# Weights that begin 64 and 192 bytes past the moving tiles: an encoder block on one Trainium2 core

## Chip, cores and metric

The kernel runs on one core of one Trainium2 chip (trn2). The metric is the device time of one execution in microseconds, taken as the median of several runs.

## What is computed

The reference is one layer of an encoder for 512 tokens of width 1024. Two token mixers, a differential attention and a neighbourhood attention, are merged by gates; then comes a feed-forward part with 2816 hidden channels. The change touches the feed-forward part, and of that its first half:

```python
x = x + rmsnorm(merged @ w_out[l], post_mix_w[l])
h = rmsnorm(x, pre_ffn_w[l])
f = (jax.nn.silu(h @ w_gate[l]) * (h @ w_up[l])) @ w_down[l]
x = x + rmsnorm(f, post_ffn_w[l])
```

All arrays are float32. The products h @ w_gate and h @ w_up are 512 x 1024 by 1024 x 2816 each.

## The kernel before

**Products in three parts.** TensorE is fed with float32r tiles. Every operand is cut into a high part (a rounded copy, made by ScalarE) and a low part (the rest, made by a subtraction on VectorE), and a product is the sum of three matmuls: high by high, high by low, low by high (`mm3`, lines 215 to 218, and lines 1109 to 1112). Each matmul has a load of 128 x 128 stationary values ahead of it, so loads and matmuls alternate one to one.

**Weights.** The class `Weights` loads a unit of weights (128 x 1024 float32, 512 KB) into one of five `raw` tiles, cuts it into the high and low part, and puts these where a place function says. Most units use `place_w` (line 197): one of four slots of the tag "w", each of 8192 bytes a partition, the high part in the first half and the low part in the second. Slots are used in turn; a slot is free again when the last matmul that reads it is done.

**Feed-forward, first blocks (UF).** Lines 1051 to 1075 multiply the first 256 gate and up columns in the usual way, 4 units with 2 halves of 256 tokens: 192 matmuls with 256 moving columns. The weights are stationary, the transposed h is moving. It stands in the two tiles of the tag "hT", which are named `Q` here (lines 925 to 929): `Q[g, n]` holds the channels 512g to 512g+511 of the tokens 256n to 256n+255, high and low part behind each other. The second half of UF needs the second half of Q, which `to_Q(h2[3], 3)` and `t_sums(1)` finish while the first half runs.

**Pair stage.** The other 20 blocks (10 gate, 10 up; 256 columns each) are computed with seven products instead of eight, in the manner of Strassen and Winograd. `pair_steps` (lines 64 to 128) makes from two weight units the stationary operands: A11 and A12 (step s0, one "w" slot, tile name "m0"), S2 and S1 (s2, one "w" slot, "s21"), S3 and S4 (s4, written over `Q[0, 1]`, which isn't needed any more, "s34"), and A22 (s5, a tile of 4096 bytes from the pool "u", "a22"). `pair_pl` (line 1033) says where each goes. The moving operands are the parts of Q (`B11`, `B21`, `B22`) and the sums T1 to T4, which are tiles of 4096 bytes of the pool "u". Each of the seven products is 12 matmuls (4 channel blocks by 3), so a block is 84 matmuls, and the stage 20 x 84 = 1680, all with 128 x 128 stationary values and 256 moving columns. For A11, A12 and A22 the low part is made by ScalarE (minus the high part) and an accumulating DMA from the queue of POOL that adds the raw weights (lines 71 to 74). The steps of the next block are dealt out between the products of the present one.

**Order.** From line 520 on a scheduler puts the instructions of each engine in order at build time; that order is then fixed.

**Addresses.** The program of before has these first bytes in a partition: slots of "w" at 18304, 26496, 34688 and 42880 (8192 each); "raw" from 51072; the 18 slots of "u" from 71552 (4096 each); the small tiles in between end at 146816, and there begin the two "hT" tiles (146816 and 163200, 16384 each). All of these are 128 modulo 256 and 384 modulo 512. Inside the tiles, parts and blocks of columns begin at multiples of 512 bytes. So every stationary operand of the pair stage begins at the same address modulo 256 as every moving one. The constants, `ident` (the moving operand of transposes) among them, begin elsewhere.

Of the kernel before, what the change touches and what calls it, by code (L numbers as in the profile page):

```python
# [9 lines left out]
F32R = mybir.dt.float32r  # L10
# [4 lines left out]
S = 512  # L15
# [17 lines left out]
def dram(ap, offset, pattern):  # L33
    return bass.AP(tensor=ap.tensor, offset=ap.offset + offset, ap=pattern)
# [143 lines left out]
def block_kernel(ctx: ExitStack, tc: tile.TileContext, x, pre_mix_w, w_in,  # L178
# [6 lines left out]
    wp = ctx.enter_context(tc.tile_pool(name="w", bufs=4))  # L185
# [7 lines left out]
    hp = ctx.enter_context(tc.tile_pool(name="hT", bufs=2))  # L193

    W = Weights(nc, rp, 5)

    def place_w():
        t = wp.tile([128, 2, 1024], F32R, tag="w", name="w")
        return t[:, 0, :], t[:, 1, :]

    def place_pool(pool):
        def go():
# [5 lines left out]
    def U(dt, shape, name, pool=None):  # L208
        return (pool or up).tile(shape, dt, tag="u", name=name)

    def cols128(w, c0, kn=KD):
        n = w.shape[1]
        return dram(w, c0, [[n, 128], [128 * n, kn], [1, 128]])
# [20 lines left out]
    for nm, c0 in (("vb", 2560), ("va", 1024)):  # L234
        for j in range(4):
            n = w_in.shape[1]
# [5 lines left out]
    def add_qk(br, i):  # L242
        qc = (1536 if br == "b" else 0) + 128 * i
        UQ[br, i, "q"] = W.add(cols128(w_in, qc), (8, 128), place_w)
        UQ[br, i, "k"] = W.add(cols128(w_in, qc + 512), (8, 128), place_w)
# [3 lines left out]
    def add_branch(nm, w, j):  # L249
        n = w.shape[1]  # L250
        src = dram(w, 256 * j, [[n, 128], [128 * n, 4], [1, 256]])
        UBR[nm, j] = W.add(src, (4, 256), place_w)
# [20 lines left out]
    UF = {}  # L273
    for m in range(2):
        for nm, w in (("g", w_gate), ("u", w_up)):
            UF[nm, m] = W.add(cols128(w, 128 * m), (8, 128), place_w)
    UP = {}
    pair_place = Late1()
    for j in range(1, KF // 2):
# [45 lines left out]
    ps_t = stk_ps.enter_context(tc.tile_pool(name="ps_t", bufs=2, space=PSUM))  # L325
    ps_o = stk_ps.enter_context(tc.tile_pool(name="ps_o", bufs=1, space=PSUM))

    hT = [hp.tile([128, 4, 2, S], F32R, tag="hT", name="hT") for _ in range(2)]
    def to_hT(h, b, dst, pool, tag):
        for g in range(2):  # L330
            tb = pool.tile([128, 4, 128], F32, tag=tag, name="tb")
            for k in range(4):
                kk = 4 * g + k
                nc.tensor.transpose(tb[:, k], h[:, 128 * kk:128 * kk + 128], ident)
            hi = dst[g][:, :, 0, 128 * b:128 * b + 128]
            lo = dst[g][:, :, 1, 128 * b:128 * b + 128]
            nc.scalar.activation(hi, tb, AF.Copy)
            nc.vector.tensor_sub(lo, tb, hi.bitcast(F32))
# [551 lines left out]
    for m in range(8):  # L890
# [16 lines left out]
        t = U(F32R, [128, 2, 512], "mg")  # L907
# [13 lines left out]
    for b in range(NB):  # L921
        t = U(F32, [128, D], "x2")
        nc.sync.dma_start(t, tok(x, b))
        x2.append(t)
    Q = {}
    for n in range(2):
        q = hp.tile([128, 2, 2, 4, 256], F32R, tag="hT", name="Q")
        for g in range(2):
            Q[g, n] = q[:, g]
    HR = {}  # L930

    def to_Q(h, b):
# [98 lines left out]
        F.append(f)  # L1031

    def pair_pl(what):
        if what == "a22":
            t = U(F32R, [128, 2, 512], "w22")
            return t[:, 0], t[:, 1]
        if what == "s34":

            return tuple(Q[0, 1][:, n].rearrange("p a b -> p (a b)") for n in range(2))
        return place_w()  # L1040

    pair_place.fn = pair_pl
    pairs = [UP[nm, j] for j in range(1, KF // 2) for nm in ("g", "u")]
# [12 lines left out]
    for half in range(2):  # L1056
        cs = slice(256 * half, 256 * half + 256)
        for m in range(2):
            for nm in ("g", "u"):
# [3 lines left out]
                for k in range(KD):  # L1063
# [3 lines left out]
                    q = Q[k // 4, half]  # L1067
# [111 lines left out]
    for b in range(NB):  # L1179
        f_split()  # L1180
        t = U(F32, [128, D], "x2")
        nc.sync.dma_start(t, x2d[b])
        x2.append(t)
    for b in range(NB):
# [6 lines left out]
        for n in range(2):  # L1191
            c = slice(512 * n, 512 * n + 512)
# [71 lines left out]
```

## Time and profile before

| | us |
|---|---|
| three runs | 753.49, 755.47, 755.78 |
| median | 755.47 |
| the profiled execution | 753.81 |
| its span, from the first to the last instruction | 752.0 |
| attention, gates and output projection, to | 398.6 |
| first feed-forward blocks (UF), to | 422.9 |
| pair stage, to | 625.0 |
| down projection and end, to | 752.0 |

The stages are told by the line numbers in the order of time: lines 216 to 218 with Q and w from 398.64 on, lines 1109 to 1112 from 422.96 to 625.2. The profile names a matmul by its line, and by out<-in with the buffer numbers left out: `b<-Th,w` is a matmul into a PSUM tile b that reads Th (moving, the high part of a T) and w (stationary). The A22 tile (`w22`) shows as w too. A matmul's duration in the trace holds the time that its results take to come out; matmuls overlap. What a matmul costs in a stream is the distance between the starts of two that follow each other.

### The profile page before, as it was taken

What the parts mean: (1) busy time and instruction counts of PE and PEld (TensorE: products, weight loads), DVE (VectorE), ACT (ScalarE), POOL (GpSimd) and SP (SyncE); (2) the same over time, 40 slices, a digit from 0 to 9 for tenths busy, and PEclk for the clock granted to TensorE, in tenths of its full rate; (3) what the DMA queues carried; (4) which work ended last, traced back from release to release, by engine and by line L of the source; (5) the groups of instructions that cost most, each with busy time, mean ns of one, the idle gap of its engine ahead of it and who ended that gap; (6) DMA issues with size and microseconds to landing.
All of it is one profiled execution on the core that took longest, in us unless ns stands there. A gap on an engine that the chain in (4) does not pass through costs nothing. (4 is left out here: it accounts for less than half of the span.)

```text
span 752.0 us, 11240 instructions
## 1 busy us (share of the span) xinstructions
PE 738.1 (98%) x4368; PEld 654.0 (87%) x4368; DVE 481.1 (64%) x840; ACT 377.2 (50%) x612; POOL 82.4 (11%) x129
## 2 busy tenths in 40 slices
PE   8999999999999999999999999999999999999996
PEld 7887888877888888887889999999999998888884
DVE  5625688888776633565467987777778879232333
ACT  6414665665666732453224865666666656222211
POOL 1001001122330000000011111111111110000000
PEclk9999999999999999999999999999999999999998
DMA  9437645333311222354714677887867872443112
GB/s 254 155 95 208 162 119 162 99 98 98 98 57 30 84 84 85 112 199 137 168 56 141 140 190 172 189 195 187 190 155 180 193 225 92 139 168 111 58 40 72
DMA packets 102582, 101.49 MB, mean 135 GB/s; under 512 B 3537, under 2 KB 85473, under 8 KB 102530
## 3 DMA queue, kind: packets, MB, share of 16 engines
q1 hardware_dynamic: 96080, 82.82, 38.2%
q0 software_dynamic: 6448, 17.97, 11.9%
q8 instruction: 34, 0.56, 0.3%
q14 instruction: 18, 0.15, 0.1%
q10 hardware_dynamic: 2, 0.00, 0.0%
HBM read 74.56 MB, written 4.19 MB: 105 GB/s over the span
## 5 line engine op out<-in xcount | busy, mean ns | idle before, releaser
L153 DVE TENSOR_TENSOR w<-raw,w 128x1024 fp32r<-128x1024 f32 x67 | 82.1, 1226 | 83.9 <-ACT w L147 83.2
L147 ACT ACTIVATE w<-raw 128x1024 fp32r<-128x1024 f32 x67 | 70.4, 1054 | 61.9 <-PE b L218 51.7
L216 PE MATMUL mm<-hT,w 128*128 128x512 f32 x256 | 100.8, 394 | 0.3 <-DVE v L391 0.3
L217 PE MATMUL mm<-hT,w 128*128 128x512 f32 x256 | 99.9, 390 | 0.0
L218 PE MATMUL mm<-hT,w 128*128 128x512 f32 x256 | 99.8, 390 | 0.0
L1109 PE MATMUL b<-Th,w 128*128 128x256 f32 x240 | 67.9, 283 | 0.0
L1111 PE MATMUL b<-Tl,w 128*128 128x256 f32 x240 | 67.9, 283 | 0.0
L1112 PE MATMUL b<-Th,w 128*128 128x256 f32 x240 | 67.9, 283 | 0.0
L216 PEld LDWEIGHTS mm<-hT,w 128*128 128x128 f32 x256 | 48.1, 188 | 10.3 <-DVE v L391 0.7
L218 PEld LDWEIGHTS mm<-hT,w 128*128 128x128 f32 x256 | 48.1, 188 | 10.3
L217 PEld LDWEIGHTS mm<-hT,w 128*128 128x128 f32 x256 | 48.1, 188 | 9.3
L216 PE MATMUL b<-w,fh 128*128 128x512 f32 x144 | 56.0, 389 | 0.0
L217 PE MATMUL b<-w,fh 128*128 128x512 f32 x144 | 56.0, 389 | 0.0
L218 PE MATMUL b<-w,fl 128*128 128x512 f32 x144 | 56.0, 389 | 0.0
L74 POOL DMA_DIRECT2D w<-raw x40 | 34.5, 862 | 174.3 <-ACT w L73 161.8
L1111 PEld LDWEIGHTS b<-Tl,w 128*128 128x128 f32 x240 | 46.1, 192 | 0.0
L1112 PEld LDWEIGHTS b<-Th,w 128*128 128x128 f32 x240 | 46.1, 192 | 0.0
L1109 PEld LDWEIGHTS b<-Th,w 128*128 128x128 f32 x240 | 46.1, 192 | 0.0
L1112 PE MATMUL b<-Q,w 128*128 128x256 f32 x160 | 45.4, 284 | 0.2 <-DMA w<-raw 0.2
L1109 PE MATMUL b<-Q,w 128*128 128x256 f32 x160 | 45.3, 283 | 0.0
L1111 PE MATMUL b<-Q,w 128*128 128x256 f32 x160 | 45.3, 283 | 0.0
L976 ACT ACTIVATE junk<-b 128x512 f32<-128x512 f32 x16 | 9.6, 597 | 61.6 <-PE b L218 56.8
(230 smaller groups left out, 1892.7 us busy)
## 6 DMA issues: line engine op xcount, KB each, us to landing
raw<-in_w_in_dram SPq DMA_DIRECT2D x40, 512.0 KB, 4.4
raw<-in_w_gate_dram SPq DMA_DIRECT2D x22, 512.0 KB, 4.3
raw<-in_w_up_dram SPq DMA_DIRECT2D x22, 512.0 KB, 4.7
raw<-in_w_down_dram SPq DMA_DIRECT2D x22, 512.0 KB, 3.3
w<-raw POOLq DMA_DIRECT2D x20, 512.0 KB, 5.7
K<-K SPq DMA_DIRECT2D x24, 256.0 KB, 3.1
w<-raw POOLq DMA_DIRECT2D x20, 256.0 KB, 5.1
x<-in_x_dram SPq DMA_DIRECT2D x8, 512.0 KB, 8.1
```

The lines of the kernel that those rows point to most:

```text
L74: nc.gpsimd.dma_start(lo, src, accum_op=ALU.add)
L147: self.nc.scalar.activation(hi, raw, AF.Copy)
L153: (engine or self.nc.vector).tensor_sub(lo, raw, hi.bitcast(F32))
L216: nc.tensor.matmul(bank, sh, mh, start=first, stop=False)
L217: nc.tensor.matmul(bank, sh, ml, start=False, stop=False)
L218: nc.tensor.matmul(bank, sl, mh, start=False, stop=last)
L976: nc.scalar.activation(junk, bs, AF.Square, scale=1.0 / 32.0, accum_out=ss[:, n:n + 1])
L1109: nc.tensor.matmul(bank[c], sh[:, k], th[:, k], start=opens and k == 0, stop=False, **kw)
L1111: nc.tensor.matmul(bank[c], sh[:, k], tl[:, k], start=False, stop=False, **kw)
L1112: nc.tensor.matmul(bank[c], sl[:, k], th[:, k], start=False, stop=k == 3, **kw)
```

## The change

No instruction is added or taken away. A slot of "w" grows by 256 bytes to 8448, an "hT" tile by 256 bytes to 16640. For the four UF units and for m0 and s21 of the pair stage, the high part begins 16 elements (64 bytes) into the slot and the low part 1072 elements (4288 bytes, 192 modulo 256). All other users of "w" have the high part at 0 and the low part at 4096, as before. Inside the two Q tiles the two groups of channels stand 2112 elements (8448 bytes, 0 modulo 256) apart, for n = 0 in the reverse order; S3 and S4 go to 16 and 1072 elements from the start of the tile for n = 1. A22 keeps its tile from "u". So modulo 256 all moving operands stay where they were, the high parts of the stationary ones of UF and of the pair stage begin 64 bytes and the low parts 192 bytes past them, and A22 begins level with them. All tiles behind the "w" slots move by 1024 bytes; as a slot is now 33 x 256 bytes, the second and fourth slot, and the second "hT" tile, begin 256 bytes off the others modulo 512. The last byte used goes from 226560 to 228096.

```diff
-    def place_w():
-        t = wp.tile([128, 2, 1024], F32R, tag="w", name="w")
-        return t[:, 0, :], t[:, 1, :]
+    def place_w(a=0, b=1024):
+
+        t = wp.tile([128, 2048 + 64], F32R, tag="w", name="w")
+        return t[:, a:a + 1024], t[:, b:b + 1024]
...
-            UF[nm, m] = W.add(cols128(w, 128 * m), (8, 128), place_w)
+            UF[nm, m] = W.add(cols128(w, 128 * m), (8, 128), lambda: place_w(16, 1072))
...
-    hT = [hp.tile([128, 4, 2, S], F32R, tag="hT", name="hT") for _ in range(2)]
+    hT = [hp.tile([128, 4160], F32R, tag="hT", name="hT")[:, :4096]
+          .rearrange("p (k a t) -> p k a t", k=4, a=2) for _ in range(2)]
...
-        q = hp.tile([128, 2, 2, 4, 256], F32R, tag="hT", name="Q")
+        q = hp.tile([128, 4160], F32R, tag="hT", name="Q")
         for g in range(2):
-            Q[g, n] = q[:, g]
+
+            c = 2112 * (1 - g) if n == 0 else 2112 * g
+            Q[g, n] = q[:, c:c + 2048].rearrange("p (a k t) -> p a k t", a=2, k=4)
+            if (g, n) == (0, 1):
+                place34 = q[:, 16:16 + 1024], q[:, 1072:1072 + 1024]
...
         if what == "s34":
-
-            return tuple(Q[0, 1][:, n].rearrange("p a b -> p (a b)") for n in range(2))
-        return place_w()
+            return place34
+        return place_w(16, 1072)
```

## Rows read from the trace of the kernel before

**Rows 1.** The page, busy time of each engine, share of the span, instructions.

```profile
PE 738.1 (98%) x4368; PEld 654.0 (87%) x4368; DVE 481.1 (64%) x840; ACT 377.2 (50%) x612; POOL 82.4 (11%) x129
```

**Rows 2.** Table by stage: stretch, its length, each engine's busy time (instructions), clock, DMA.

```profile
398.60:422.90 24.30, 24.12 (x201) 23.87 (x201) 22.26 (x36) 15.29 (x25) 3.79 (x5) 1.00 0.50 135
422.90:625.00 202.10, 201.90 (x1682) 201.69 (x1682) 160.13 (x242) 127.62 (x170) 32.66 (x38) 1.00 0.79 188
625.00:752.00 127.00, 119.95 (x530) 99.00 (x529) 46.46 (x51) 32.98 (x44) 2.18 (x4) 0.98 0.29 95
```

**Rows 3.** Timeline, pair stage: start, duration, engine, line, what; one block to the next.

```profile
524.24 0.28 PE L1109 MATMUL b<-Q,w 128*128 128x256 f32 x1
...
534.33 0.28 PE L1109 MATMUL b<-Q,w 128*128 128x256 f32 x1
...
534.57 0.28 PE L1112 MATMUL b<-Q,w 128*128 128x256 f32 x1
```

**Rows 4.** Timeline, down projection, matmuls with 512 columns, first and last of 31.

```profile
699.90 0.39 PE L216 MATMUL b<-w,fh 128*128 128x512 f32 x1
...
706.70 0.39 PE L216 MATMUL b<-w,fh 128*128 128x512 f32 x1
```

**Rows 5.** Timeline, a weight load in the same stretch of the pair stage.

```profile
524.25 0.19 PEld L1111 LDWEIGHTS b<-Q,w 128*128 128x128 f32 x1
```

**Rows 6.** Timeline, the first matmuls of UF, the first two and the twelfth.

```profile
398.64 0.28 PE L216 MATMUL b<-Q,w 128*128 128x256 f32 x1
398.75 0.28 PE L217 MATMUL b<-Q,w 128*128 128x256 f32 x1
...
399.95 0.28 PE L218 MATMUL b<-Q,w 128*128 128x256 f32 x1
```

**Rows 7.** Timeline, matmuls with 256 columns in the attention stage.

```profile
169.02 0.28 PE L707 MATMUL o<-pl,v 128*128 128x256 f32 x1
169.13 0.29 PE L706 MATMUL o<-ph,v 128*128 128x256 f32 x1
169.26 0.28 PE L707 MATMUL o<-pl,v 128*128 128x256 f32 x1
169.37 0.28 PE L706 MATMUL o<-ph,v 128*128 128x256 f32 x1
```

**Rows 8.** Timeline, matmuls with 512 columns after other work, the first three and the sixth.

```profile
182.83 0.39 PE L216 MATMUL mm<-hT,w 128*128 128x512 f32 x1
183.06 0.40 PE L217 MATMUL mm<-hT,w 128*128 128x512 f32 x1
183.30 0.39 PE L218 MATMUL mm<-hT,w 128*128 128x512 f32 x1
...
183.99 0.39 PE L218 MATMUL mm<-hT,w 128*128 128x512 f32 x1
```

**Rows 9.** Four transposes: timeline (merged), and their group (busy us, mean ns).

```profile
182.16 0.60 PE L784 MATMUL t<-ident,p 128*128 128x128 f32 x4
...
L784 PE MATMUL t<-ident,p 128*128 128x128 f32 x64 | 9.9, 274 | 0.0
```

**Rows 10.** Groups of the page: count, busy us, mean ns, idle before.

```profile
L216 PE MATMUL mm<-hT,w 128*128 128x512 f32 x256 | 100.8, 394 | 0.3 <-DVE v L391 0.3
...
L216 PE MATMUL b<-w,fh 128*128 128x512 f32 x144 | 56.0, 389 | 0.0
```

**Rows 11.** The two waits of TensorE in the stretch (timeline), and the chain between them.

```profile
411.47 0.39 PE L217 MATMUL b<-Q,w 128*128 128x256 f32 x1 [0.18 <-DVE Q L943]
432.21 0.39 PE L1112 MATMUL b<-Q,w 128*128 128x256 f32 x1 [0.20 <-DMA w<-raw]
...
425.56 6.61 DMA w<-raw
```

**Rows 12.** The accumulating DMAs: one issue (timeline), and landing times of all 40.

```profile
521.13 0.86 POOL L74 DMA_DIRECT2D w<-raw  x1 [6.15 <-ACT w L73]
...
DMA to landing us min/median/max: 3.9/5.6/6.9
```

## Prediction

> **What bounds the kernel now.** I read the page's busy shares first. TensorE is busy 98% of the span [rows 1]. Then the table by stage: the granted clock is 1.00 there, so the upper of its two levels, 2.4 GHz; and in the stretch that the change touches, 398.6 to 625 us, TensorE is idle for 0.4 us of 226.4, and the weight loads fill as much of the time [rows 2]. VectorE (79% of the pair stage), ScalarE (63%) and the DMA engines (0.79) have room. So the stage costs its number of matmuls times the distance from one matmul's start to the next, and nothing but that distance, the pitch, can be won or lost there in any amount.
>
> The pitch comes from start times. From the first matmul of one gate or up block at 524.24 to the same one of the next block at 534.33 lie 84 matmuls: 10.09 / 84 = 0.1201 us; 534.33 to 534.57 are two single steps of 0.12 [rows 3]. In the stage of the down projection, 30 steps with 512 columns take 706.70 - 699.90 = 6.80 us, 0.2267 each [rows 4]. 256 more columns thus cost 106.6 ns, 0.416 ns each, one column per cycle of 2.4 GHz. What 256 columns need alone is 106.6 ns; the other 13.5 ns come with every matmul, at 512 columns (226.7 - 213.2 = 13.5) as at 256.
>
> These 13.5 ns are what the change aims at. During a matmul the weights of the next one are loaded: a load starts within 0.01 us of a matmul's start [rows 3, 5]. Both read SBUF. By the layout of the kernel before, every stationary and every moving float32r tile of the pair stage begins at the same address modulo 256, so here the two reads always start in step; the trace before holds no sustained run at another offset.
>
> **Does the pitch depend on anything but the column count?** Yes, and this is my reason to expect an effect. The same 256-column form does 0.11 for its first step after the 512-column stage and 1.31 / 11 = 0.1191 over the first eleven [rows 6]; in the attention stage three steps in a row are 0.11, 0.13 and 0.11 [rows 7]. After other work the 512-column form does 0.23, 0.24 and three more of 0.23 in the mean (0.232 over the five) before it falls to its lasting 0.2267, with no wait between [rows 8]. A fixed charge for changing weights would not wander by 10 ns; two streams that meet more or less often, according to how they stand to each other, would. An offset moves exactly that standing.
>
> Four transposes of 128 columns show the floor: the row spans 0.60 us, the last one lasts 0.274, so three steps take 0.326, 109 ns each [rows 9]. Their moving part needs only 128 x 0.416 = 53 ns, so 109 ns is the weight load's own pace, and no offset can bring a stream of load and matmul below it.
>
> **The change, part by part.** No instruction is added, removed or moved to another engine. All costs are start addresses.
> 1. New offsets in the pair stage: 1680 matmuls (20 blocks of 84; the window in rows 2 has two of the stage before besides) less the 240 on A22, whose tile stays as it was, so 1440; and the 192 matmuls of the first two feature blocks (UF), together 1632. The price of an offset of 64 or 192 bytes is in no row. Its ends are 109 ns (11 less than now, rows 9) and 125 ns (5 more: the step of 0.13 in rows 7 between two of 0.11, taken at the low end of its rounding). Between them I take 115 ns, 5 less than now: the nearest rows for the same form are the first steps of 0.11 in rows 6 and 7, which are lower than 120 but not sustained, so I take half of the way to the floor.
> 2. Not all of the 1632 can give their 5 ns to the end. The 97 UF matmuls ahead of 411.47 (the first half of 96 and one more) end in a wait for VectorE's chain to Q (0.18 us now); that chain doesn't hang on them, so what they win turns into waiting [rows 11]. Behind it, 169 shifted matmuls up to 432.21 (95 of UF, 74 of the pair stage) run against ScalarE and the accumulating DMAs on POOL's queue: the wait at 432.21 is for such a DMA, issued at 425.56 and there 6.6 us later [rows 11]. That chain starts when TensorE frees a weight slot, so it moves along in part; I count half. Counted in full are 1440 + 192 - 97 - 169 = 1366; with half of 169 it is 1450. 1450 x 5 ns = 7.25 us.
> 3. Slots of 8448 bytes: the offsets of the other stages stay 0 modulo 256, but every second weight slot moves by 256 modulo 512. About half of the 3 x 256 feature matmuls on w and of the 3 x 144 of the down stage [rows 10] are met, 600. No row isolates this; if they ran 0.230 instead of 0.2267, as in rows 8, it would be 3.3 ns x 600 = 2 us, and I know no reason against the opposite sign. Taken at 0, both ends kept.
> 4. The addresses that ScalarE, VectorE and the DMA write: their instructions move as much as before. The accumulating DMA is the only one with little cover at the start (point 2). Later it has plenty: the one issued at 521.13 takes 6.9 us at the longest, so it is there by 528.0, and its low parts are first used by the third matmul of the next block at 534.57 [rows 3, 12]; 6 us are left, and a block that is 0.4 us shorter takes none of this cover away. SyncE's queue gets no new wait.
> 5. VectorE needs 160.13 / 202.1 of the pair stage; if the stage fell to 195, 82%, and at the floor of 109 ns 87%. It doesn't become the bound.
>
> Sum: against the profiled execution, 753.81 us (span 752.0 and 1.8 around it), 753.81 - 7.25 = 746.6. The median of the three runs, 755.47, lies 1.66 above that execution, so the forecast is 748.2.
>
> **A rule that speaks against it.** The Trainium skill, page "SBUF — State Buffer", section "Who interferes with whom", gives TensorE two independent read ports, one for the moving operand and one for the weights, and says that it never waits on anyone; by this no address can matter, and the sum would be 755.5. The page "TensorE: Matmul & The Clock Gate", "Back-to-back issue gap", puts the step at N/2.4 + 2.5, so 109.2 ns for 256 columns, an estimate from that page; the trace has 120.1, and doesn't agree. The wandering steps of rows 6 to 8 don't either.
>
> **The rivals.**
> - *No effect.* The 13.5 ns is the same for 256 and 512 columns [rows 3, 4], as a fixed charge per change of weights would be, and the wandering is only the settling of a pipeline after a break. Then any offset gives 120 ns and the change does nothing: 755.5, 753.5 to 757.5 with point 3. Against it: rows 6 to 8.
> - *All of it goes.* The meetings vanish and the weight load alone sets the pace, 109 to 110 ns: 10.5 x 1450 = 15.2 us, 740.2; with all 1632 and 11 ns, 18 us, 737.5. For it: the transposes hold 109 [rows 9]. Against: in rows 6 and 7 each step of 0.11 has a longer one behind it, and the mean stays at 0.119.
> - *Slower: a worse standing.* The settled pitch at offset 0 could be a good one, and the new offsets put the load where the moving read runs into it longer, at each matmul. Rows 8 speak for it: there the unsettled 512-column steps are longer than the settled one; rows 6 and 7 speak against, since at 256 columns they average less than 120. It decides from 121.4 ns on (1632 x 1.4 ns = 2.3 us). No cover exists, as TensorE has no idle time; at 124 ns it is 1632 x 4 = 6.5 us, 762.0; at 122.5, 4.1 us, 759.6.
>
> **How the numbers follow.** A measurement of this kernel tells about 0.3%, 2.3 us, from no change. Forecast (pitch 111 to 118.4, 743 to 753): 0.42. All of it: 0.18. No effect: 0.22. Slower: 0.18. Faster is 0.42 + 0.18 = 0.60, same 0.22, slower 0.18. For the range I go down to 738, which leaves out 0.06 of the floor case, and up to 760, which leaves out 0.10 of the slower case. The likeliest case's own range is 743 to 753.
>
> **What would show it.** Right: between equal matmuls of two blocks 84 steps take about 9.7 us instead of 10.09; the blocks on A22 (12 matmuls each, offset unchanged) still go at 0.12, right beside blocks at less; weight loads keep their 0.19 us; the down stage keeps 0.2267; the wait for Q at 411.5 grows to some 0.7 us and the one for the DMA at 432 to about 0.5. Steps of 0.12 everywhere would show the no-effect rival; steps of 0.11 everywhere the floor; steps of 0.12 and 0.13 mixed, the slower one. The prediction is wrong if TensorE starts to wait in the pair stage (then the next bound was nearer than points 4 and 5 say), or if the 512-column stages change their step (point 3).

## The result, and the profile after

The changed kernel takes 749.5 us (median of 4 runs, 748.3 to 750.0) against 754.5 for the kernel before (4 runs). The medians lie 5.0 us apart, 0.7%; the ratio of the runs is put at 0.992, with a 95% interval of 0.990 to 0.994. Its profiled execution took 748.33 us with a span of 746.6, 5.5 less than the one of before.

The table by stage, with the borders of the changed kernel's own trace (same columns as rows 2; the first stretch is UF, the second the pair stage, the third the rest):

```profile
398.81:422.55 23.74, 22.97 (x202) 22.77 (x201) 21.86 (x36) 14.74 (x25) 3.79 (x5) 1.00 0.49 134
422.55:619.61 197.06, 195.41 (x1683) 193.44 (x1682) 160.43 (x243) 128.00 (x172) 32.67 (x38) 1.00 0.81 190
619.61:746.60 126.99, 119.86 (x530) 98.91 (x528) 46.46 (x51) 32.90 (x44) 2.18 (x4) 0.99 0.30 100
```

UF falls from 24.3 to 23.7 us, the pair stage from 202.1 to 197.1, the rest stays. TensorE now idles for 1.65 us of the pair stage, where it idled for 0.2.

Now the steps (timeline, columns as in rows 3). First the 24 matmuls of S2 and S1 in one block, then the 12 of A22 a little later:

```profile
522.92 0.28 PE L1116 MATMUL b<-Th,w 128*128 128x256 f32 x1
...
525.53 0.28 PE L1119 MATMUL b<-Th,w 128*128 128x256 f32 x1
...
530.07 0.28 PE L1116 MATMUL b<-Th,w 128*128 128x256 f32 x1
...
531.39 0.28 PE L1119 MATMUL b<-Th,w 128*128 128x256 f32 x1
```

23 steps take 2.61 us, 113.3 ns each in the trace's unrounded times; the 11 steps of A22, whose weights begin level with the moving tile as before, take 1.32 us, 120 ns. The second half of UF, from 412.57 to 422.32, does 86 steps in 9.75 us, 113.3 ns again. So where the offset changed, the lasting step fell by 6.7 ns, from 120.0 to 113.3, and nowhere else. The down stage keeps 0.2267.

Taken over the 1632 shifted matmuls that is 10.9 us, of which UF and the pair stage together gave 5.6. The other 5.3 went into waits, and into steps that had not yet settled. The waits of TensorE's weight loads, from UF on (who waited for whom, us in total, times, longest):

```profile
PEld b L1116 <- DVE pv L1126: 2.1, 8, 0.3
PEld b L1119 <- DMA w<-raw: 1.5, 2, 1.1
PEld b L218 <- DVE Q L949: 1.0, 1, 1.0
```

The lower two are those of rows 11, grown, with one more of their kind. In the timeline of TensorE:

```profile
411.65 0.38 PE L218 MATMUL b<-Q,w 128*128 128x256 f32 x1 [0.77 <-DVE Q L949]
423.09 0.39 PE L1119 MATMUL b<-Q,w 128*128 128x256 f32 x1 [0.16 <-DMA w<-raw]
432.47 0.39 PE L1119 MATMUL b<-Q,w 128*128 128x256 f32 x1 [0.93 <-DMA w<-raw]
```

TensorE comes earlier, and the chain to Q on VectorE and the accumulating DMAs do not: counted from the start of UF, the matmul that waits for Q starts after 12.8 us in both traces, and the one that waits for the DMA after 33.6 before and 33.7 after. The first line of the waits is new: eight times, in every second block, S4 waits for line 1126, VectorE's addition that reads the bank of S1. S4 adds into that same bank. One such place, TensorE and VectorE side by side:

```profile
526.89 0.28 PE L1119 MATMUL b<-Th,Q 128*128 128x256 f32 x1
527.23 0.38 PE L1116 MATMUL b<-Q 128*128 128x256 f32 x1
527.45 0.28 PE L1118 MATMUL b<-Q 128*128 128x256 f32 x1
527.57 0.28 PE L1119 MATMUL b<-Q 128*128 128x256 f32 x1
...
525.83 0.41 DVE L1124 TENSOR_TENSOR pv<-pv,b 128x256 f32<-128x256 f32 x1
526.16 0.69 DVE L107 TENSOR_TENSOR S<-raw,S 128x512 f32<-128x512 f32 x1
526.76 0.41 DVE L1126 TENSOR_TENSOR pv<-pv,b 128x256 f32<-128x256 f32 x1
```

S3 ends, VectorE reads the bank until 527.17, and S4 starts at 527.23. From 526.89 to 527.45 pass 0.56 us for two steps that would need 0.23. In the trace of before, the same addition (line 1119 there) was already late, by a hair. At one of the eight places:

```profile
468.94 0.42 DVE L1119 TENSOR_TENSOR pv<-pv,b 128x256 f32<-128x256 f32 x1
469.26 0.19 PEld L1112 LDWEIGHTS b<-Th,Q 128*128 128x128 f32 x1
469.41 0.19 PEld L1109 LDWEIGHTS b<-Q 128*128 128x128 f32 x1
469.50 0.30 PE L1109 MATMUL b<-Q 128*128 128x256 f32 x1
469.64 0.28 PE L1111 MATMUL b<-Q 128*128 128x256 f32 x1
```

The addition ends at 469.36, and S4's first weight load starts 0.15 us after the load ahead of it instead of 0.12. S4 lost 18 ns there, eight times.

Worked out over every step from the start of UF to the end of the pair stage, what goes beyond 113.3 ns (shifted) and 120 ns (level) comes to 6.2 us after and 1.0 us before, transposes left out. After, it is 2.7 us at the three early waits and in the step behind the transposes of UF (1.0 before), 2.7 us at the eight waits at S4 (0.15 before), and 0.8 us in steps that take a while to fall back to their lasting pace after a wait or after A22.

### The profile page after: what moved, and what is told of

It reads as the page before. It is cut to its first block, busy times and chain, and to the rows that moved or that the text cites. A ratio compares the mean times of both kernels' runs of the same rounds, so it can differ in the third digit from the quotient of the medians.

```text
span 746.6 us, 11240 instructions
## 1 busy us (share of the span) xinstructions
PE 730.4 (98%) x4368; PEld 644.6 (86%) x4368; DVE 481.1 (64%) x840; ACT 376.9 (50%) x612; POOL 82.5 (11%) x129
## 5 line engine op out<-in xcount | busy, mean ns | idle before, releaser
L1116 PE MATMUL b<-Th,w 128*128 128x256 f32 x240 | 66.8, 278 | 0.0
L1119 PE MATMUL b<-Th,w 128*128 128x256 f32 x240 | 66.8, 278 | 0.0
L1119 PE MATMUL b<-Q,w 128*128 128x256 f32 x160 | 44.5, 278 | 1.1 <-DMA w<-raw 1.1
L1119 PEld LDWEIGHTS b<-Th,w 128*128 128x128 f32 x240 | 45.4, 189 | 0.0
L1116 PEld LDWEIGHTS b<-Th,w 128*128 128x128 f32 x240 | 45.3, 189 | 0.0
L1118 PE MATMUL b<-Q,w 128*128 128x256 f32 x160 | 44.3, 277 | 0.0
L1116 PE MATMUL b<-Q,w 128*128 128x256 f32 x160 | 44.3, 277 | 0.0
```

The costliest lines, as they stand in the source:

```text
L1116: nc.tensor.matmul(bank[c], sh[:, k], th[:, k], start=opens and k == 0, stop=False, **kw)
L1118: nc.tensor.matmul(bank[c], sh[:, k], tl[:, k], start=False, stop=False, **kw)
L1119: nc.tensor.matmul(bank[c], sl[:, k], th[:, k], start=False, stop=k == 3, **kw)
```

## Experiments

Four of them exchange two products, which is said there; all others keep the changed kernel's order of work and differ in start addresses alone. The stage ahead of UF, which most edits don't touch, took between 398.6 and 400.7 us in the profiled executions, so I compare lengths of stages and steps rather than whole times where a kernel ran once.

**The offset undone, all else kept.** The slots of 8448 bytes and the new places of Q stay.

```diff
-    lambda: place_w(16, 1072)         # UF
+    lambda: place_w(0, 1024)
-            if (g, n) == (0, 1): place34 = q[:, 16:16 + 1024], q[:, 1072:1072 + 1024]
+            if (g, n) == (0, 1): place34 = q[:, 0:0 + 1024], q[:, 1024:1024 + 1024]
-        return place_w(16, 1072)      # m0, s21
+        return place_w(0, 1024)
```

> The changed kernel with its larger slots, its Q layout and its order of work, but with the high and low parts of UF, m0, s21 and s34 back at 0 and 4096 bytes, level with the moving tiles modulo 256. Theory (the step depends on how far the weights begin past the moving tile): steps of 0.120 us in the whole pair stage, 84 steps in 10.08 us, the pair stage 202 us, the time that of the kernel before within 0.3%, 753 to 757. Rival (the slots of 8448 bytes, which put tiles 256 bytes apart modulo 512, make the gain): steps of 0.113 stay, about 749.5.

Measured: 754.9 us, ratio to before 1.001 (0.999 to 1.002). The same stretch as above (S2 and S1 of one block):

```profile
527.01 0.28 PE L1116 MATMUL b<-Th,w 128*128 128x256 f32 x1
...
529.77 0.28 PE L1119 MATMUL b<-Th,w 128*128 128x256 f32 x1
```

2.76 us for 23 steps, 120.0 ns; the pair stage is back at 202.4 us. The gain is the offset's. The slots and the 256 bytes modulo 512 that they bring are worth nothing that can be measured.

**Is it the distance, or the address of the weights?** Here high and low parts stand 64 bytes into their slots, and Q is moved by 64 bytes as well.

```diff
-    lambda: place_w(16, 1072)         # UF; m0, s21 and place34 likewise
+    lambda: place_w(16, 1040)
-            c = 2112 * (1 - g) if n == 0 else 2112 * g
+            c = 16 + (2048 * (1 - g) if n == 0 else 2048 * g)
```

> All stationary high and low parts of UF, m0, s21 and s34 begin 64 bytes into their slots, and the moving Q tiles are moved by 64 bytes too, so that the weights are level with Q and 64 bytes past the T tiles. Theory (the distance between weights and moving tile counts): products with Q (UF, A11, A12, S4) step at 0.120 us, products with T (S1, S2, S3) at 0.113, A22 with T4 at 0.120, all in one run: a block of 84 takes 4 x 12 x 0.120 + 3 x 12 x 0.113 = 9.84 us. Rival (the address of the weights alone counts): 0.113 everywhere but for A22. Rival (high and low parts must stand 128 bytes apart): 0.120 everywhere.

Measured: one run of 752.1 us, pair stage 199.2. First UF (weights level with Q), then S2 and S1 (64 bytes past T):

```profile
413.66 0.28 PE L219 MATMUL b<-Q,w 128*128 128x256 f32 x1
...
423.98 0.28 PE L218 MATMUL b<-Q,w 128*128 128x256 f32 x1
...
525.37 0.29 PE L1116 MATMUL b<-Th,w 128*128 128x256 f32 x1
...
527.99 0.28 PE L1119 MATMUL b<-Th,w 128*128 128x256 f32 x1
```

86 steps in 10.32 us are 120.0 ns; 23 steps in 2.62 us are 113.9 (the first few of each T run are longer, then they settle at 113.3). The weights are at the same addresses modulo 256 in both, so their address alone doesn't set the step; nor does that of the moving tile alone, since T, at the same address modulo 256, gives 120.0 when the weights are level (the run above) and 113.3 here. The distance decides. Within a block, A12 does 120.0 throughout; A11 and S4, which follow products with another distance, do 119.2 and 118.6 in the mean. And the low parts need no offset of their own: 64 bytes for every load does the same as 64 and 192.

**Other offsets.** Two runs with an offset for the high and another for the low parts, two with one offset for every load with T and another for every load with Q. The edits are those above with other numbers (8 and 1048; 32 and 1080; 32 and 1056 with Q moved by 8 elements; 8 and 1032 with Q moved by 24; in the last two an "hT" tile grows by another 256 bytes).

> High parts 32 bytes, low parts 96 bytes past the moving tiles modulo 256. Theory: the step is set by the offset, one value for each; these two lie either side of 64, so if 64 is good because the streams are then clear of each other by a margin, both keep 0.113 us; if the gain is tied to multiples of 64, steps of 0.120 or a mixture come back and the stage goes up to 200 us. Rival (any offset other than 0 does): 0.113 for all but the A22 products, pair stage 197 us. Rival (the slots make the gain): 0.113.

> High parts 128 bytes, low parts 224 bytes past the moving tiles modulo 256. Theory with a period of 128 bytes: 128 is as good as level, so loads of high parts go with steps of 0.120 us, and 224 (96 modulo 128) as in the run with 32 and 96. Theory with a period of 256: 128 is the farthest from level, steps of 0.113 or less, down to the 0.109 of the transposes. Rival (any offset other than 0 does): 0.113.

> One offset at a time: high and low parts both 128 bytes into their slots, and the Q tiles moved by 32 bytes, so that products with T (S1, S2, S3) have 128 bytes for every load, and products with Q (UF, A11, A12, S4) 96 bytes. Theory with a period of 128 bytes: the steady step with T is 0.120 us as when level; with Q it lies between 0.113 and 0.120. Theory with a period of 256: the step with T is 0.113 or less, down to 0.109.

> One offset at a time again: high and low parts both 32 bytes into their slots, the Q tiles moved by 96 bytes, so that products with T (S1, S2, S3) have 32 bytes for every load and products with Q (UF, A11, A12, S4) 192 bytes. Theory (64 and 192 are good by themselves, not as a pair of high and low): steady steps of 0.113 us with Q, 0.117 to 0.118 with T, as the high parts had in the run with 32 and 96. Rival (192 is good only for the low parts, between loads of high parts at 64): 0.116 to 0.120 with Q.

Measured, with the means over the second half of UF and over S2 and S1 of one block (unrounded start times); the first two times are medians of several runs, the others single runs:

| offset of the loads, bytes | steps with Q (UF) ns | steps with T ns | pair stage us | time, us |
|---|---|---|---|---|
| level (the run above) | 120.0 | 120.0 | 202.4 | 754.9 |
| high 64, low 192 (the change) | 113.3 | 113.3 | 197.1 | 749.5 |
| high 32, low 96 | 117.7 | 117.8 | 200.0 | 751.6 |
| high 128, low 224 | 119.9 | 120.2 | 201.8 | 754.6 |
| Q: 96, T: 128 | 117.3 | 118.8 | 200.8 | 753.3 |
| Q: 192, T: 32 | 117.8 | 118.2 | 200.4 | 753.9 |

The timeline of the last line's run, first and last step of the stretch from which its column for Q comes:

```profile
414.44 0.28 PE L219 MATMUL b<-Q,w 128*128 128x256 f32 x1
...
424.56 0.28 PE L218 MATMUL b<-Q,w 128*128 128x256 f32 x1
```

10.12 us for 86 steps, where 113.3 ns a step would take 9.75. My theory fell here: 192 by itself is not good. It does no harm to the low parts, which are loaded between loads of high parts at 64, but alone it gives 117.8. Neither period holds either: 128 is not level (118.8 and not 120.0) and not good. At level and at 64 every settled step is the same; at the others the single steps go between 113 and 124 ns. They don't come to one value, but in UF they come to a pattern that repeats: with 128 and 224 the unrounded steps go 117, 123, 120 and again, with 192 alone they are 117 to 119 in a round of nine. What makes 64 settle lower than level these runs don't show. That stays open.

**Where the rest of the gain went.** A12 with B21 is put ahead of S4 with B22, and the step that writes the next S3 and S4 comes one product later.

```diff
-             ("S3", "T3", "D", "c22"), ("S4", "B22", "C", "c12"), ("A12", "B21", "A", "c11"),
+             ("S3", "T3", "D", "c22"), ("A12", "B21", "A", "c11"), ("S4", "B22", "C", "c12"),
...
-            if nxt and i in ((0, 1, 2, 4, 5) if n else (1, 2, 3, 5, 6)):
+            if nxt and i in ((0, 1, 2, 5, 6) if n else (1, 2, 3, 5, 6)):
```

> The changed kernel with two of the seven products exchanged: A12 with B21 before S4 with B22, and the steps of the next block that write S3 and S4 dealt out one product later. Theory (in every second block TensorE waits at S4, because S4 adds into the bank of S1, which VectorE has not yet read out while it is busy with the two products of ff_out): the eight waits of 0.34 us at S4 go, 2.7 us, 749.5 to about 746.8. Rival (VectorE is the bound of these blocks, whatever the order): the eight waits come back at A12, A22 or the next block, and the time stays within 748.5 to 750.5.

Measured: 746.0 us, ratio to before 0.989 (0.987 to 0.991). The pair stage, and all that is left of the waits of the weight loads from 425 us on:

```profile
424.32:617.96 193.64, 192.87 (x1682) 192.48 (x1681) 158.12 (x243) 126.84 (x172) 32.67 (x38) 1.00 0.83 196
...
PEld b L1119 <- DMA w<-raw: 1.2, 2, 0.8
```

The stage is 3.4 us shorter, and none of the eight waits is left; they didn't come back elsewhere. VectorE was late at one place in the order, and not the bound. The 3.4 is more than the waits' own 2.7: 0.4 are the steps behind them that had wandered, and 0.3 the two early waits for a DMA, which were shorter in this run. This is the fastest version of the study.

**The same offsets for the stages with 512 columns.** `place_w` gets other defaults, so that the matmuls of the attention stage's projections, of the gates and of the down projection are shifted as well; the pair stage keeps 64 and 192.

```diff
-    def place_w(a=0, b=1024):
+    def place_w(a=16, b=1072):        # 64 and 192; (32, 1056): 128; (16, 1040): 64
```

> The changed kernel with the offsets of 16 and 1072 elements for every user of the w slots, so that also the matmuls with 512 columns have weights and moving tile 64 or 192 bytes apart (feature stage, branch products, down projection; about 1500 matmuls). Theory (each weight load costs the moving stream 13.3 ns when level and 6.7 ns at 64 or 192, whatever the number of columns): steps fall from 0.2267 to 0.220 us, 1500 x 6.7 ns = 10 us, about 739.5. Rival (at 512 columns the load is done half way, so it never sets the step, and the charge there is fixed): 0.2267 stays, 748 to 751.

> Both of the two runs beside it at once, offsets for all users of the w slots and the exchanged products. Theory: the gains add, 749.5 - 10 - 2.7 = 736.8. Rival (one of them doesn't carry): that of the other alone, 739.5 or 746.8.

> The run with the exchanged products, and in the stages with 512 columns both parts of the w slots 128 bytes from level (the pair stage keeps 64 and 192). Theory (at 512 columns the level start is the one that settles, and every other offset keeps wandering): steps of 0.229 to 0.233 us there, the time 2 to 6 us above the 746.0 of the run with the exchange alone. Rival (128 is as level, or better): 0.2267 or less, 738 to 746.

> The run with the exchanged products, and in the stages with 512 columns both parts of the w slots 64 bytes from level: in the feature stage weights 64 bytes past the moving hT for every load, in the down stage the moving w 64 bytes past the weights, which is 192 the other way. Theory (64 bytes for every load is an offset that settles, at 512 columns as at 256): 0.220 us in the feature stage, about 800 x 6.7 ns = 5 us there, and 0.229 to 0.233 in the down stage. Rival (at 512 columns only the level start settles): 0.229 to 0.233 in both, 749 to 753.

Measured: 753.2 us with 64 and 192 (ratio to before 0.999, 0.997 to 1.000), 751.3 with these and the exchange (0.995, 0.994 to 0.997), and single runs of 751.3 with 128 and 753.7 with 64 for every load, both with the exchange. Each is slower than the same kernel with these stages level, 749.5 without and 746.0 with the exchange. Of the four expectations only that of the run with 128 came out; in place of the gains of 10 and 5 us there were losses. A stretch of the gate stage without interruption, in the changed kernel (level) and then in the run with 64 for every load; 357 steps each:

```profile
270.15 0.39 PE L219 MATMUL mm<-hT,w 128*128 128x512 f32 x1
...
351.10 0.39 PE L219 MATMUL b<-ya,w 128*128 128x512 f32 x1
```

```profile
273.14 0.40 PE L219 MATMUL mm<-hT,w 128*128 128x512 f32 x1
...
356.45 0.39 PE L219 MATMUL b<-ya,w 128*128 128x512 f32 x1
```

80.95 us against 83.31, 226.8 ns a step against 233.4. With 64 and 192 the gate stage has 231.9, with 128 it has 232.4. In the down stage the step is 230.4 with 64 and 192, 232.4 with 128, and 233.3 in the run with 64, where it is the moving tile that begins 64 bytes past the weights:

```profile
635.57 0.40 PE L219 MATMUL b<-w,fl 128*128 128x512 f32 x1
...
705.57 0.40 PE L219 MATMUL b<-w,fl 128*128 128x512 f32 x1
```

These are 300 steps in 70.00 us. So at 512 columns the theory of a charge per load that depends on the offset alone fell: level is the best of the four there, and 64, which gave 113.3 at 256 columns, the worst.

## Why the prediction was right

1. *TensorE's step is what the stage costs.* Right. The shorter step less the waits is the gain, and the 512-column stages kept theirs.
2. *The step hangs on how the two reads stand to each other.* Right: undoing the offset brings 120.0 back, and moving Q along with the weights brings it back for the products with Q alone. That the two reads meet and hold each other up, as the prediction pictures it, is not shown; shown is that the distance sets the step. The 13.5 ns are no fixed charge: at 64 bytes they became 6.7 at 256 columns and 20.0 at 512. The no-effect rival gave 755.5. The rule of the Trainium skill that TensorE's two read ports are independent and that it never waits on anyone ("SBUF — State Buffer", "Who interferes with whom") led the prediction to the same time; the measured 749.5 and these two runs disagree with what was drawn from it. The 109.2 ns that the prediction takes from the Trainium skill's page "TensorE: Matmul & The Clock Gate" ("Back-to-back issue gap") is, by that section, the gap of a matmul by itself, so it was no forecast for a stream in which each matmul has a weight load.
3. *Its size, 5 ns, for 115 ns.* The mis-sized term: 6.7 ns, 113.3. The unsettled steps of 0.11 in rows 6 and 7 were nearer to the truth than the half-way value that I took. A block without a wait took 9.61 us where some 9.7 had been forecast.
4. *Gain lost ahead of 432 us.* Right in its places, too small in its size. I had 0.9 us (182 matmuls by 5 ns); the early waits took 1.8 us more than before. The wait for Q came out as forecast (0.77 against "some 0.7"), the one at 432 at 0.93 instead of 0.5, and the wait at 423.09 I had not seen coming.
5. *VectorE and the queues keep up.* This step failed. I had held VectorE's busy share (82%) against the shorter stage, and that was the wrong test: it showed that VectorE would not be the bound, and it wasn't, but one of its additions came at a point of the order where it was already 0.02 us late. In rows 2 this can't be seen; the eight steps of 138 to 140 ns at the start of S4 in the trace of before showed it. It cost 2.6 us. By the prediction's own sign of being wrong, TensorE starting to wait in the pair stage, the next bound was nearer than its points 4 and 5 say.
6. *The sum.* 748.2 for 749.5. Against the profiled execution, 7.25 us forecast and 5.5 measured; between the medians 5.0, since the forecast counted from 755.5 and the four runs of before have 754.5. Points 3 and 5 missed in opposite directions, 2.7 us too little (1632 by 1.67 ns) and 2.6 too much; the forecast lies as near as it does because these two cancel, and that is luck. What is left of the difference is 0.8 us in point 4, 0.8 us of steps that were slow to settle, and 0.2 us ahead of UF.
7. *Slots of 8448 bytes at nothing.* Right: 754.9 with them alone. The slower rival had its mechanism right for another place: at 512 columns the level start is the good standing and the shifted one costs up to 6.7 ns a step.

## What to carry to other kernels

Where matmuls and weight loads alternate and TensorE never idles, measure the step from start to start and compare it with the columns alone; what is above can depend on the distance of the two operands' start addresses, and a kernel can try that without touching its order. Try it for each column count by itself, since 64 bytes, among the best at 256 columns, was the worst of four at 512. And before counting a shorter step in full, list each dependency of the stage that is met or missed by a small margin, not only the busy shares: here half of the gain went into two kinds of them and the steps behind them, and exchanging two products brought 3.4 of the 5.3 us back.

## What the hardware showed that I had not expected

One column takes 0.417 ns, from the difference of the level steps at 512 and 256 columns (226.7 and 120.0), so 256 columns alone take 106.7 ns and 512 take 213.3. The lasting steps stand in even distances above that: 6.7 ns (113.3), 13.3 (120.0 and 226.7) and 20.0 (233.3), which are 16, 32 and 48 cycles at the granted 2.4 GHz. In the down stage every step of the run with 64 is 232 to 234 ns; in its gate stage steps of about 231 and 236 take turns, with the same mean. The other offsets gave no single lasting step, but steps that change from matmul to matmul, 113 to 124 ns at 256 columns, with means from 117.3 to 120.2. The runs don't say why.
